# Pairwise products of the forget gates made in the projection stage, and two norms with fewer operations

## The chip, the cores and the metric

The kernel runs on one NeuronCore of a Trainium2 chip. The metric is the device time of one execution in microseconds (us); the time before is the median of three runs. Engines are named as in the profile: PE is TensorE, PEld its weight loads, DVE VectorE, ACT ScalarE, POOL GpSimd and SP SyncE, whose queue issues nearly all DMAs.

## The reference, cut to what matters

One step of a hybrid backbone of two layers, for 2048 latent and 256 context tokens (2304 in all, width 1024). A layer normalises and modulates its input, projects it, runs four mixers (differential attention, S5, HGRN2 and latent attention, MLA), gates them and projects back. The change touches HGRN2's gates, and the norm and the softmax of MLA:

```python
log_f = jnp.log(lb + (1.0 - lb) * jax.nn.sigmoid(z))   # forget gate f, per head, channel, direction
k = (1.0 - lb) * jax.nn.sigmoid(-z)
...
b = jnp.cumsum(gc, axis=1)
decay = jnp.exp(jnp.where(causal, b[:, :, None] - b[:, None, :], -jnp.inf))
scores = jnp.einsum("bthd,btshd,bshd->bhts", qc, decay, kc)
...
q = (rms_norm(cq) * P["mla_q_norm"][l].astype(F32)).astype(dt) @ P["mla_w_uq"][l]
ckv_n = (rms_norm(ckv) * P["mla_kv_norm"][l].astype(F32)).astype(dt)
...
p = jax.nn.softmax(s, axis=-1).astype(v.dtype)
return jnp.einsum("bhqk,bkhd->bqhd", p, v)
```

The decay between two tokens of a chunk of 64 is the product of the gates between them.

## The kernel before

Both layers run the same stages. `first_stage` projects keys, queries and values of differential attention (`proj1`, blocks of 384 tokens). In `mixers`, `proj2` makes the rest of the projection in four token groups of 576, each in two halves of 288 columns; it is woven with the differential attention that is already running, and TensorE's order in it is that of the program text. Then the remaining attention (differential, then MLA) is woven with `ssm()`, that is HGRN and after it S5. `out_proj` closes the layer. Outside TensorE's order in `proj2` a planner orders each engine's queue, by its own costs and by priorities; it places an operation as soon as its inputs are there by its reckoning, and the engines then issue in that order.

In `proj2` the blocks of `FB2` go one after another: 24 matmuls of 288 columns for each half, then `evac2`. Four of the blocks are `hf`, a head's gate pre-activations of both directions (64 + 64 rows). Line 393 clamps them out of PSUM, lines 394 to 396 are ScalarE's, line 397 makes k and line 398 the gate f in the tile `evf`, which goes to the DRAM tensor `HF` (line 399); k goes to `PF` (line 403). GpSimd meanwhile splits the next block's weights into a high and a low part (`split2`, lines 171 and 173).

`mla_up` in the same stage norms by `rs_bc`: a sum of squares by matmul, a logarithm and an exponential on ScalarE, one Newton step on VectorE (lines 594 to 597).

`hgrn` takes a head in five groups of up to 512 tokens (40 groups over two layers; the last of a head has 256). A group loads F (the gates, line 1035), X and Y (q and k of both directions). The decay inside a chunk of 64 is made by doubling: at level `lev` blocks of 2^lev tokens are paired, the second block's X and the first block's Y are multiplied by a gate product of the other block (lines 1059, 1060), and `T2`, made from the pairs of `T` (line 1062), is the gate product of the joined block. The six products of a group are a chain of their own: they need F alone. The last goes into `td` (lines 1095, 1096) for the scan over the chunks. Three groups can be in flight (`HB`).

MLA's second pass divides by the sum of the exponentials with one Newton step (lines 984 to 989). S matrices of the attention rotate through four PSUM banks.

Of the kernel before, what the change touches and what calls it, by code (L numbers as in the profile page):

```python
# [10 lines left out]
F32 = mybir.dt.float32  # L11
# [5 lines left out]
ALU = mybir.AluOpType  # L17
# [9 lines left out]
NT = LS + LC  # L27
# [79 lines left out]


PR = (0, 0)
AVB = 2  # L110
PPB = 3
DA_A = 740
# [269 lines left out]
def evac2(g, l, p, kind, idx, ps, tok0, n):  # L382
    nc = g.nc
    sl = slice(tok0, tok0 + n)
    o = p.tile([128, n], F32, tag="ev", name="ev", bufs=EVB)
    if kind == "u":
        nc.scalar.copy(o.rearrange("p (s j) -> p s j", s=8), ps.rearrange("p (j s) -> p s j", s=8))
        nc.sync.dma_start(g.UD[idx * 128:(idx + 1) * 128, :, tok0 // 8:(tok0 + n) // 8], o.rearrange("p (s j) -> p s j", s=8))
        return
    if kind == "hf":  # L390
        om, lb = g.omlb[:, l, idx:idx + 1], g.lb[:, l, idx:idx + 1]
        f = p.tile([128, n], F32, tag="evf", name="evf")
        nc.vector.tensor_scalar(o, ps, -80.0, None, ALU.max)
        nc.scalar.activation(out=o, in_=o, func=AF.Exp, scale=-1.0)
        nc.scalar.activation(out=f, in_=o, func=AF.Ln, bias=1.0)
        nc.scalar.activation(out=f, in_=f, func=AF.Exp, scale=-1.0)
        nc.vector.scalar_tensor_tensor(o, o, om, f, ALU.mult, ALU.mult)
        nc.vector.tensor_scalar(f, f, om, lb, ALU.mult, ALU.add)
        nc.sync.dma_start(g.HF[idx, :, sl], f)
    else:  # L400
        nc.scalar.copy(o, ps)
    dst, r0 = (g.GX, GIDX[kind] + idx * 128) if kind in GIDX else (g.PF, FROW[(kind, idx)])
    nc.sync.dma_start(dst[r0:r0 + 128, sl], o)
# [102 lines left out]
def proj2(g, l):  # L506
    nc = g.nc
    G, H = 576, 288
    with ExitStack() as es:
        pa = es.enter_context(pool(g, "p2a", 1, "right"))  # L510
        p = es.enter_context(pool(g, "p2", 2, "right"))
        ph = es.enter_context(pool(g, "p2h", 1, "right"))
        pu = es.enter_context(pool(g, "mu", 1, "right"))
        for t0 in range(0, NT, G):
            hi, lo = [], []
            for b in range(2):
                bs = slice(t0 + b * H, t0 + (b + 1) * H)
                for j, x in enumerate((hi, lo)):
                    t = (pa, ph)[b].tile([128, 8, H], F32R, tag=f"h{j}{b}", name="h2")
# [3 lines left out]
                if b == 0 and t0 == 0:  # L523
                    yield GS0
                    w = mla_up_weights(g, l, ph)
# [37 lines left out]

            def ups():
                if t0 == 0:
                    ck = pu.tile([128, H], F32, tag="ckc", name="ckc")
                    nc.sync.dma_start(ck[:, :256], g.A["cmc"][l])
                    yield from mla_kv(g, l, w, pu, ck, NT, 256)
                for b in range(2):
                    yield from mla_up(g, l, w, pu, cks[b], cqs[b], t0 + b * H, H)  # L570
# [11 lines left out]
def rs_bc(g, p, sqs, n, inv_n):  # L582
    nc = g.nc
    ps = pst(g, "mm", "psrb")
    for i, s in enumerate(sqs):
        k = s.shape[0]
        nc.tensor.matmul(ps[:, :n], lhsT=g.ones[:k, :], rhs=s, start=(i == 0), stop=(i == len(sqs) - 1))
    a = p.tile([128, 288], F32, tag="rba", name="rba")[:, :n]
    y = p.tile([128, 288], F32, tag="rby", name="rby")[:, :n]
    t = p.tile([128, 288], F32, tag="rbt", name="rbt")[:, :n]  # L590
    nc.vector.tensor_scalar(a, ps[:, :n], inv_n, EPS, ALU.mult, ALU.add)
    nc.scalar.activation(out=y, in_=a, func=AF.Ln)
    nc.scalar.activation(out=y, in_=y, func=AF.Exp, scale=-0.5)
    nc.vector.tensor_tensor(t, y, y, ALU.mult)
    nc.vector.tensor_tensor(t, t, a, ALU.mult)
    nc.vector.tensor_scalar(t, t, -0.5, 1.5, ALU.mult, ALU.add)
    nc.vector.tensor_tensor(y, y, t, ALU.mult)
    return y


# [287 lines left out]
def mla(g, l, p):  # L888
    nc = g.nc
# [46 lines left out]
    def pass2(pr, qb):  # L936
        n, _, kts = key_blocks(qb)
# [4 lines left out]
        av = pst(g, "av", "psmav")  # L942
# [39 lines left out]
        rc = g.pm.tile([128, 512], F32, tag="mrc", name="mrc")  # L982
        tq = g.pm.tile([128, 512], F32, tag="mtq", name="mtq")
        nc.scalar.activation(out=rc[:, :n], in_=pd[:, :n], func=AF.Ln)
        nc.scalar.activation(out=rc[:, :n], in_=rc[:, :n], func=AF.Exp, scale=-1.0)
        nc.vector.tensor_tensor(tq[:, :n], pd[:, :n], rc[:, :n], ALU.mult)
        nc.vector.tensor_scalar(tq[:, :n], tq[:, :n], -1.0, 2.0, ALU.mult, ALU.add)
        nc.vector.tensor_tensor(rc[:, :n], rc[:, :n], tq[:, :n], ALU.mult)
        nc.vector.tensor_tensor(rc[:, :n], av[:, :n], rc[:, :n], ALU.mult)
        nc.sync.dma_start(g.MX[768 + pr * 128:768 + (pr + 1) * 128, qb * 512:qb * 512 + n], rc[:, :n])  # L990
        yield 1

# [3 lines left out]
def hgrn(g, l, p, p1):  # L996
    nc = g.nc
# [10 lines left out]
    for xs, n, nm in ((ks, 6, "hks"), (qz, 2 * HB, "hqz")):  # L1008
        for i in range(n):
            t = p1.tile([128, 512], F32, name=f"{nm}{i}")  # L1010
# [19 lines left out]
    def group(k, h, c0, nch):  # L1030
# [2 lines left out]
        r0, z0 = FROW[("hq", h // 2)] + (h % 2) * 64, FROW[("hf", h)]  # L1033
        F, X, Y = (p.tile([128, 512], F32, tag=t, name="h" + t, bufs=n)[:, :W] for t, n in (("F", 3), ("X", HB), ("Y", HB)))
        nc.sync.dma_start(F, g.HF[h, :, sl])
        nc.sync.dma_start(Y[0:64], g.PF[z0:z0 + 64, sl])
        nc.sync.dma_start(X[64:128], g.PF[z0 + 64:z0 + 128, sl])
        nc.sync.dma_start(X[0:64], g.PF[r0:r0 + 64, sl])
# [6 lines left out]
        nc.vector.tensor_tensor(X[0:64], X[0:64], F[0:64], ALU.mult)  # L1045
        nc.vector.tensor_tensor(Y[64:128], Y[64:128], F[64:128], ALU.mult)
        nc.vector.tensor_tensor(Av, ps[:, :W // 2].rearrange("p (c t) -> p c t", t=64), g.id64.unsqueeze(1).to_broadcast([128, nch, 64]), ALU.mult)
        T = F
        for lev in range(6):
            m = 1 << lev  # L1050
            nb = W // (2 * m)
            K_, Q_ = ks[lev], qz[k % HB * 2 + lev % 2]
            xx, yy, kz, qq = (t_[:, :W].rearrange("p (b t m) -> p b t m", t=2, m=m) for t_ in (X, Y, K_, Q_))
            nc.scalar.copy(kz[0:64, :, 0, :], yy[0:64, :, 0, :])
            nc.scalar.copy(kz[64:128, :, 1, :], xx[64:128, :, 1, :])
            nc.scalar.copy(qq[0:64, :, 1, :], xx[0:64, :, 1, :])
            nc.scalar.copy(qq[64:128, :, 0, :], yy[64:128, :, 0, :])
            Tv = T.rearrange("p (b t) -> p b t", t=2)
            nc.vector.tensor_tensor(xx[:, :, 1, :], xx[:, :, 1, :], Tv[:, :, 0:1].to_broadcast([128, nb, m]), ALU.mult)
            nc.vector.tensor_tensor(yy[:, :, 0, :], yy[:, :, 0, :], Tv[:, :, 1:2].to_broadcast([128, nb, m]), ALU.mult)  # L1060
            T2 = p.tile([128, 256 >> lev], F32, tag=f"T{lev}", name=f"T{lev}")[:, :nb]
            nc.vector.tensor_tensor(T2, Tv[:, :, 0], Tv[:, :, 1], ALU.mult)
            T = T2
            ps = pst(g, "mm", "pshg")
            pairs(ps, K_, Q_, nch)
            nc.vector.copy_predicated(Av, g.masks[:, lev, :].bitcast(U32).unsqueeze(1).to_broadcast([128, nch, 64]),
                                      ps[:, :W // 2].rearrange("p (c t) -> p c t", t=64))
            yield 2.5
        nc.scalar.copy(QF[0:64, sl], X[0:64])
        nc.scalar.copy(QF[64:128, sl], Y[64:128])  # L1070
        pt = pst(g, "mm", "pskt")
# [624 lines left out]
def build(nc, tc, A, O, depth=DEPTH):  # L1696
    with ExitStack() as es:
# [7 lines left out]
        g.ED = dp.tile([2, 128, 16, 257], F32, name="ED")  # L1705
        g.X1 = dp.tile([NT, D], F32, name="X1")
        g.PF = dp.tile([1120, NT], F32, name="PF")
        g.HF = dp.tile([4, 128, NT], F32, name="HF")
        g.GX = dp.tile([D, NT], F32, name="GX")
        g.KRD = dp.tile([2, 34, NK], F32, name="KRD")  # L1710
# [97 lines left out]
```

## Time and profile before

| what | value |
|---|---|
| median of three runs | 5299.3 us (5298.6 to 5303.79) |
| profiled execution, its own time | 5296.69 us |
| its span, first to last instruction | 5294.9 us |
| mean granted TensorE clock | 0.935 |
| TensorE, VectorE, ScalarE, GpSimd busy | 89%, 72%, 60%, 21% |

The profile is of one execution. The stages of layer 0 lie at 0 to 464 us (`first_stage`), 464 to 1537 (`proj2` with attention), 1537 to 2056 (HGRN with attention), 2056 to 2380 (S5 with attention) and from there to 2716 (the end of the attention and `out_proj`); those of layer 1 begin at 2716, 3097, 4184, 4686 and 4973. Busy time is the time in which an engine executes; its idle time costs something only where it lies on the chain of work that ended last.

### The profile page before, as it was taken

What the parts mean: (1) busy time and instruction counts of PE and PEld (TensorE: products, weight loads), DVE (VectorE), ACT (ScalarE), POOL (GpSimd) and SP (SyncE); (2) the same over time, 40 slices, a digit from 0 to 9 for tenths busy, and PEclk for the clock granted to TensorE, in tenths of its full rate; (3) what the DMA queues carried; (4) which work ended last, traced back from release to release, by engine and by line L of the source; (5) the groups of instructions that cost most, each with busy time, mean ns of one, the idle gap of its engine ahead of it and who ended that gap; (6) DMA issues with size and microseconds to landing.
All of it is one profiled execution on the core that took longest, in us unless ns stands there. A gap on an engine that the chain in (4) does not pass through costs nothing.

```text
span 5294.9 us, 81097 instructions
## 1 busy us (share of the span) xinstructions
PE 4724.9 (89%) x27920; PEld 3434.4 (65%) x27920; DVE 3835.7 (72%) x7616; ACT 3183.3 (60%) x7516; POOL 1089.4 (21%) x1323
## 2 busy tenths in 40 slices
PE   6787999999998997898987879999999989989899
PEld 5676767677665664445776757676776656654477
DVE  7655767676668886896676657676766688879877
ACT  3225878777777783235433258787777777743354
POOL 4651222222210000000227712222222100000022
PEclk8998999999998997899999989999999989989999
DMA  6555233433332124415445452334333321241253
GB/s 219 170 174 154 87 105 96 130 116 104 92 88 75 47 57 129 130 50 148 157 155 200 159 167 86 108 94 130 116 103 93 88 73 48 54 117 52 75 155 126
DMA packets 507523, 599.37 MB, mean 113 GB/s; under 512 B 147630, under 2 KB 414806, under 8 KB 507110
## 3 DMA queue, kind: packets, MB, share of 16 engines
q1 hardware_dynamic: 506630, 592.61, 37.3%
q8 instruction: 220, 3.60, 0.3%
q14 instruction: 193, 1.58, 0.1%
q0 software_dynamic: 480, 1.57, 0.1%
HBM read 378.42 MB, written 215.18 MB: 112 GB/s over the span
## 4 chain that ended last, share of the span: by engine, by line
PE 49%; DVE 18%; DMA 13%; ACT 10%; issue 4%; POOL 4%; SPq 1%; ACTq 0%; DVEq 0%; POOLq 0%
PE psav L858 5%; PE psS L870 4%; PE psF L177 4%; PE psF L178 4%; PE psF L179 4%; PE psS L817 4%; PE psmav L950 3%; ACT junk L820 3%; PE psM L961 2%; DVE nm L818 2%; DVE a L872 2%; DVE mnm L927 2%; ACT pp L871 2%; PE psM L926 2%; PE pshg L1018 2%
## 5 line engine op out<-in xcount | busy, mean ns | idle before, releaser
L818 DVE TENSOR_REDUCE nm<-psS 128x1 f32<-128x512 f32 (+1 forms) x1312 | 790.5, 626 | 351.7 <-PE psS L817 340.5
L820 ACT ACTIVATE junk<-psS,nm 128x512 bf16<-128x512 f32 (+1 forms) x1312 | 848.7, 647 | 202.2 <-DVE nm L818 182.4
L871 ACT ACTIVATE pp<-psS 128x512 f32<-128x512 f32 (+1 forms) x1184 | 654.5, 594 | 165.7 <-PE psS L870 159.6
L177 PE MATMUL psF<-h,whi 128*128 128x288 f32 x2304 | 697.9, 303 | 32.8 <-ACT whi L169 32.8
L872 DVE SCALAR_TENSOR_TENSOR a<-pp,nlam 128x512 f32<-128x512 f32 (+1 forms) x592 | 510.3, 864 | 257.6 <-ACT pp L871 256.9
L178 PE MATMUL psF<-h,whi 128*128 128x288 f32 x2304 | 687.9, 299 | 0.0
L179 PE MATMUL psF<-h,wlo 128*128 128x288 f32 x2304 | 685.1, 297 | 1.8 <-DVE wlo L173 1.8
L964 ACT ACTIVATE me<-psM 128x512 f32<-128x512 f32 (+1 forms) x592 | 345.6, 590 | 440.8 <-PE psM L963 395.1
L817 PE MATMUL psS<-ks,qs 96*128 96x512 f32 (+1 forms) x1312 | 544.5, 425 | 58.9 <-ACT junk L820 37.7
L870 PE MATMUL psS<-qs,ks 98*128 98x512 f32 (+1 forms) x1184 | 440.6, 436 | 53.9 <-ACT junk L820 38.7
L177 PEld LDWEIGHTS psF<-h,whi 128*128 128x128 f32 x2304 | 444.7, 193 | 65.3 <-ACT whi L169 34.5
L171 POOL CAST whi<-w 128x1024 fp32r<-128x1024 f32 x140 | 153.2, 1094 | 1622.0 <-PE psF L178 1299.7
L178 PEld LDWEIGHTS psF<-h,whi 128*128 128x128 f32 x2304 | 444.8, 193 | 54.8
L927 DVE TENSOR_REDUCE mnm<-psM 128x1 f32<-128x512 f32 (+1 forms) x656 | 394.1, 623 | 70.9 <-PE psM L926 69.0
L179 PEld LDWEIGHTS psF<-h,wlo 128*128 128x128 f32 x2304 | 441.5, 192 | 3.1 <-DVE wlo L173 3.1
L817 PEld LDWEIGHTS psS<-ks,qs 96*128 96x128 f32 x1312 | 255.2, 197 | 165.5 <-ACT junk L820 98.4
L870 PEld LDWEIGHTS psS<-qs,ks 98*128 98x128 f32 x1184 | 203.3, 192 | 236.3 <-ACT junk L820 136.4
L173 POOL TENSOR_TENSOR wlo<-w,whi 128x1024 fp32r<-128x1024 f32 x140 | 350.3, 2502 | 11.2
L967 DVE TENSOR_TENSOR macc<-macc,me 128x1024 f32<-128x1024 f32 x256 | 311.2, 1216 | 45.0 <-ACT me L964 44.2
L950 PE MATMUL psmav<-me,mv 128*64 128x512 f32 (+1 forms) x1184 | 318.0, 631 | 13.7 <-ACT me L964 7.9
L858 PE MATMUL psav<-a,dav 128*64 128x512 f32 (+1 forms) x1184 | 309.5, 643 | 18.2 <-DVE a L872 18.2
L961 PE MATMUL psM<-qs,ks 98*128 98x512 f32 (+1 forms) x592 | 269.8, 456 | 49.2 <-ACT me L964 21.6
(451 smaller groups left out, 10191.2 us busy)
## 6 DMA issues: line engine op xcount, KB each, us to landing
w<-wF SPq DMA_DIRECT2D x152, 512.0 KB
h<-HD SPq DMA_DIRECT2D x64, 576.0 KB
wmod<-w_mod SPq DMA_DIRECT2D x48, 512.0 KB
HD<-hhi SPq DMA_DIRECT2D x12, 1536.0 KB
HD<-hlo SPq DMA_DIRECT2D x12, 1536.0 KB
GX<-ev SPq DMA_DIRECT2D x128, 144.0 KB
gt<-GX SPq DMA_DIRECT2D x36, 512.0 KB
PF<-ev SPq DMA_DIRECT2D x96, 144.0 KB
```

What stands on the lines that cost most here:

```text
L177: nc.tensor.matmul(out, lhsT=w_hi, rhs=x_hi, start=start, stop=False)
L178: nc.tensor.matmul(out, lhsT=w_hi, rhs=x_lo, start=False, stop=False)
L179: nc.tensor.matmul(out, lhsT=w_lo, rhs=x_hi, start=False, stop=stop)
L817: nc.tensor.matmul(ps[:, :kn], lhsT=qs[0:96, i, t * 128:(t + 1) * 128], rhs=key_cols(ks[i], k0, kn)[0:96], start=True, stop=True)
L818: nc.vector.tensor_reduce(nm[:, i, t, ci:ci + 1], ps[:, :kn], axis=AX.X, op=ALU.max, negate=True)
L820: nc.scalar.activation(out=junk[:, :kn], in_=ps[:, :kn], func=AF.Exp, bias=nm[:, i, t, ci:ci + 1], accum_out=sm[:, i, t, ci:ci + 1])
L858: x = nc.tensor.matmul(av[hh * 64:(hh + 1) * 64, :n], lhsT=v[:, kt, hh * 64:(hh + 1) * 64], rhs=aa[:, hh, :n], start=(ki == 0), stop=(ki = ...
L870: nc.tensor.matmul(ps[:, :n], lhsT=key_cols(ks[2 * hh + m], kt * 128, 128), rhs=qs[:, 2 * hh + m, :n], start=True, stop=True)
L871: nc.scalar.activation(out=pp[:, m, :n], in_=ps[:, :n], func=AF.Exp)
L872: last = nc.vector.scalar_tensor_tensor(aa[:, hh, :n], pp[:, 1, :n], nlam, pp[:, 0, :n], ALU.mult, ALU.add)
L927: nc.vector.tensor_reduce(nm[:, i, t, ci:ci + 1], ps[:, :kn], axis=AX.X, op=ALU.max, negate=True)
L950: x = nc.tensor.matmul(av[i * 64:(i + 1) * 64, :n], lhsT=v[:, kts[ki], i * 64:(i + 1) * 64], rhs=e[:, i, :n], start=(ki == 0), stop=(ki == ...
```

## The change

Of the six gate products of a group, those of levels 0 to 4 are made in `evac2`, right behind the gate f, for 288 tokens at a time: five dependent VectorE operations with 144, 72, 36, 18 and 9 results in each partition, in a tile `evt` with one buffer. They are stored in a new DRAM tensor `HT`, in rows of 31 numbers for each 32 tokens. `hgrn` loads them with each group into a tile with two buffers (`HTB`) and keeps only the last product, from the 16 numbers in place 30. In `rs_bc` and in MLA's second pass three operations are written as two, with SCALAR_TENSOR_TENSOR. The tile `ckc` shares the buffer of `sq2`.

```diff
--- before.py
+++ after.py
@@ -107,6 +107,7 @@
 
 
 PR = (0, 0)
+HTB = 2
 AVB = 2
 PPB = 3
 DA_A = 740
@@ -397,6 +398,14 @@
         nc.vector.scalar_tensor_tensor(o, o, om, f, ALU.mult, ALU.mult)
         nc.vector.tensor_scalar(f, f, om, lb, ALU.mult, ALU.add)
         nc.sync.dma_start(g.HF[idx, :, sl], f)
+        nb = n // 32
+        tt = p.tile([128, nb, 32], F32, tag="evt", name="evt", bufs=1)
+        src, a = f.rearrange("p (k c) -> p k c", c=32), 0
+        for w in (16, 8, 4, 2, 1):
+            s2 = src.rearrange("p k (b t) -> p k b t", t=2)
+            nc.vector.tensor_tensor(tt[:, :, a:a + w], s2[:, :, :, 0], s2[:, :, :, 1], ALU.mult)
+            src, a = tt[:, :, a:a + w], a + w
+        nc.sync.dma_start(g.HT[idx, :, tok0 // 32:tok0 // 32 + nb, 0:31], tt[:, :, 0:31])
     else:
         nc.scalar.copy(o, ps)
     dst, r0 = (g.GX, GIDX[kind] + idx * 128) if kind in GIDX else (g.PF, FROW[(kind, idx)])
@@ -563,7 +572,7 @@
 
             def ups():
                 if t0 == 0:
-                    ck = pu.tile([128, H], F32, tag="ckc", name="ckc")
+                    ck = pu.tile([128, 2, H], F32, tag="sq2", name="ckc")[:, 0, :]
                     nc.sync.dma_start(ck[:, :256], g.A["cmc"][l])
                     yield from mla_kv(g, l, w, pu, ck, NT, 256)
                 for b in range(2):
@@ -592,9 +601,8 @@
     nc.scalar.activation(out=y, in_=a, func=AF.Ln)
     nc.scalar.activation(out=y, in_=y, func=AF.Exp, scale=-0.5)
     nc.vector.tensor_tensor(t, y, y, ALU.mult)
-    nc.vector.tensor_tensor(t, t, a, ALU.mult)
-    nc.vector.tensor_scalar(t, t, -0.5, 1.5, ALU.mult, ALU.add)
-    nc.vector.tensor_tensor(y, y, t, ALU.mult)
+    nc.vector.scalar_tensor_tensor(t, t, -0.5, a, ALU.mult, ALU.mult)
+    nc.vector.scalar_tensor_tensor(y, t, 1.5, y, ALU.add, ALU.mult)
     return y
 
 
@@ -984,9 +992,8 @@
         nc.scalar.activation(out=rc[:, :n], in_=pd[:, :n], func=AF.Ln)
         nc.scalar.activation(out=rc[:, :n], in_=rc[:, :n], func=AF.Exp, scale=-1.0)
         nc.vector.tensor_tensor(tq[:, :n], pd[:, :n], rc[:, :n], ALU.mult)
-        nc.vector.tensor_scalar(tq[:, :n], tq[:, :n], -1.0, 2.0, ALU.mult, ALU.add)
-        nc.vector.tensor_tensor(rc[:, :n], rc[:, :n], tq[:, :n], ALU.mult)
-        nc.vector.tensor_tensor(rc[:, :n], av[:, :n], rc[:, :n], ALU.mult)
+        nc.vector.scalar_tensor_tensor(rc[:, :n], tq[:, :n], 2.0, rc[:, :n], ALU.subtract, ALU.mult)
+        nc.vector.scalar_tensor_tensor(rc[:, :n], av[:, :n], -1.0, rc[:, :n], ALU.mult, ALU.mult)
         nc.sync.dma_start(g.MX[768 + pr * 128:768 + (pr + 1) * 128, qb * 512:qb * 512 + n], rc[:, :n])
         yield 1
 
@@ -1033,6 +1040,8 @@
         r0, z0 = FROW[("hq", h // 2)] + (h % 2) * 64, FROW[("hf", h)]
         F, X, Y = (p.tile([128, 512], F32, tag=t, name="h" + t, bufs=n)[:, :W] for t, n in (("F", 3), ("X", HB), ("Y", HB)))
         nc.sync.dma_start(F, g.HF[h, :, sl])
+        ht = p.tile([128, 16, 32], F32, tag="ht", name="hht", bufs=HTB)[:, :W // 32]
+        nc.sync.dma_start(ht[:, :, 0:31], g.HT[h, :, c0 * 4:c0 * 4 + W // 32, 0:31])
         nc.sync.dma_start(Y[0:64], g.PF[z0:z0 + 64, sl])
         nc.sync.dma_start(X[64:128], g.PF[z0 + 64:z0 + 128, sl])
         nc.sync.dma_start(X[0:64], g.PF[r0:r0 + 64, sl])
@@ -1045,7 +1054,6 @@
         nc.vector.tensor_tensor(X[0:64], X[0:64], F[0:64], ALU.mult)
         nc.vector.tensor_tensor(Y[64:128], Y[64:128], F[64:128], ALU.mult)
         nc.vector.tensor_tensor(Av, ps[:, :W // 2].rearrange("p (c t) -> p c t", t=64), g.id64.unsqueeze(1).to_broadcast([128, nch, 64]), ALU.mult)
-        T = F
         for lev in range(6):
             m = 1 << lev
             nb = W // (2 * m)
@@ -1055,17 +1063,25 @@
             nc.scalar.copy(kz[64:128, :, 1, :], xx[64:128, :, 1, :])
             nc.scalar.copy(qq[0:64, :, 1, :], xx[0:64, :, 1, :])
             nc.scalar.copy(qq[64:128, :, 0, :], yy[64:128, :, 0, :])
-            Tv = T.rearrange("p (b t) -> p b t", t=2)
-            nc.vector.tensor_tensor(xx[:, :, 1, :], xx[:, :, 1, :], Tv[:, :, 0:1].to_broadcast([128, nb, m]), ALU.mult)
-            nc.vector.tensor_tensor(yy[:, :, 0, :], yy[:, :, 0, :], Tv[:, :, 1:2].to_broadcast([128, nb, m]), ALU.mult)
-            T2 = p.tile([128, 256 >> lev], F32, tag=f"T{lev}", name=f"T{lev}")[:, :nb]
-            nc.vector.tensor_tensor(T2, Tv[:, :, 0], Tv[:, :, 1], ALU.mult)
-            T = T2
+            if 0 < lev < 5:
+                a, w = 32 - (64 >> lev), 32 >> lev
+                Tv = ht[:, :, a:a + w].rearrange("p k (b t) -> p k b t", t=2)
+                xk, yk = (t_.rearrange("p (k b t m) -> p k b t m", k=W // 32, t=2, m=m) for t_ in (X, Y))
+                x1, y0 = xk[:, :, :, 1, :], yk[:, :, :, 0, :]
+                ta, tb = (Tv[:, :, :, i:i + 1].to_broadcast([128, W // 32, w // 2, m]) for i in range(2))
+            else:
+                Tv = (F if lev == 0 else ht[:, :, 30]).rearrange("p (b t) -> p b t", t=2)
+                x1, y0 = xx[:, :, 1, :], yy[:, :, 0, :]
+                ta, tb = (Tv[:, :, i:i + 1].to_broadcast([128, nb, m]) for i in range(2))
+            nc.vector.tensor_tensor(x1, x1, ta, ALU.mult)
+            nc.vector.tensor_tensor(y0, y0, tb, ALU.mult)
             ps = pst(g, "mm", "pshg")
             pairs(ps, K_, Q_, nch)
             nc.vector.copy_predicated(Av, g.masks[:, lev, :].bitcast(U32).unsqueeze(1).to_broadcast([128, nch, 64]),
                                       ps[:, :W // 2].rearrange("p (c t) -> p c t", t=64))
             yield 2.5
+        T = p.tile([128, 8], F32, tag="T5", name="T5")[:, :2 * nch]
+        nc.vector.tensor_tensor(T, Tv[:, :, 0], Tv[:, :, 1], ALU.mult)
         nc.scalar.copy(QF[0:64, sl], X[0:64])
         nc.scalar.copy(QF[64:128, sl], Y[64:128])
         pt = pst(g, "mm", "pskt")
@@ -1705,6 +1721,7 @@
         g.ED = dp.tile([2, 128, 16, 257], F32, name="ED")
         g.X1 = dp.tile([NT, D], F32, name="X1")
         g.PF = dp.tile([1120, NT], F32, name="PF")
+        g.HT = dp.tile([4, 128, NT // 32, 32], F32, name="HT")
         g.HF = dp.tile([4, 128, NT], F32, name="HF")
         g.GX = dp.tile([D, NT], F32, name="GX")
         g.KRD = dp.tile([2, 34, NK], F32, name="KRD")
```

## Rows read from the trace of the kernel before

**Rows 1.** The page: each engine's busy time, and the chain by engine.

```profile
PE 4724.9 (89%) x27920; PEld 3434.4 (65%) x27920; DVE 3835.7 (72%) x7616; ACT 3183.3 (60%) x7516; POOL 1089.4 (21%) x1323
...
PE 49%; DVE 18%; DMA 13%; ACT 10%; issue 4%; POOL 4%; SPq 1%; ACTq 0%; DVEq 0%; POOLq 0%
```

**Rows 2.** Stretches: busy us of each engine, granted clock, DMA share, GB/s.

```profile
464.00:1537.00 1073.00, 996.14 (x5389) 756.22 (x5391) 737.44 (x1265) 822.75 (x2170) 252.48 (x141) 0.96 0.34 103
1537.00:2056.00 519.00, 475.59 (x4061) 311.79 (x4059) 417.57 (x962) 385.68 (x881) 9.10 (x15) 0.91 0.23 61
4686.00:4973.00 287.00, 258.00 (x1020) 135.66 (x1018) 271.13 (x534) 94.19 (x171) 0.71 (x7) 0.96 0.27 75
```

**Rows 3.** The same view: two of the eight stretches with `hf`.

```profile
525.00:594.00 69.00, 62.89 (x346) 49.52 (x344) 56.48 (x90) 55.30 (x144) 19.53 (x12) 0.98 0.29 91
1063.00:1130.00 67.00, 62.20 (x366) 50.38 (x365) 52.74 (x103) 53.89 (x152) 18.66 (x11) 1.00 0.51 149
```

**Rows 4.** Timeline, HGRN stage: start us, us, engine, line, operation.

```profile
1593.14 0.28 DVE L1062 TENSOR_TENSOR T<-T 128x128 f32<-128x128 f32 x1
...
1595.00 0.21 DVE L1062 TENSOR_TENSOR T<-T 128x64 f32<-128x64 f32 x1
...
1596.48 0.18 DVE L1062 TENSOR_TENSOR T<-T 128x32 f32<-128x32 f32 x1
...
1598.20 0.17 DVE L1062 TENSOR_TENSOR T<-T 128x16 f32<-128x16 f32 x1
...
1599.39 0.15 DVE L1062 TENSOR_TENSOR T<-T 128x8 f32<-128x8 f32 x1
```

**Rows 5.** Timeline in an `hf` stretch: GpSimd and VectorE.

```profile
534.65 2.72 POOL L173 TENSOR_TENSOR wlo<-w,whi 128x1024 fp32r<-128x1024 f32 x1
...
535.03 2.50 DVE L398 TENSOR_SCALAR evf<-evf,omlb,lb 128x288 f32<-128x288 f32 x1
```

**Rows 6.** Single lines: ns as min/median/max, first and last start.

```profile
L397 DVE SCALAR_TENSOR_TENSOR ev<-ev,omlb,evf x64: 498/509/1811, 532.2 to 4033.5; 128x288 f32<-128x288 f32 x64
...
L398 DVE TENSOR_SCALAR evf<-evf,omlb,lb x64: 407/428/2499, 535.0 to 4034.3; 128x288 f32<-128x288 f32 x64
...
L595 DVE TENSOR_TENSOR rbt<-rbt,rba x32: 444/458/2548, 530.4 to 4138.9; 128x288 f32<-128x288 f32 x32
L596 DVE TENSOR_SCALAR rbt<-rbt x32: 292/309/1031, 530.9 to 4139.4; 128x288 f32<-128x288 f32 x32
```

**Rows 7.** Groups, 464 to 1537 us: busy us, mean ns | idle before.

```profile
L397 DVE SCALAR_TENSOR_TENSOR ev<-ev,omlb,evf 128x288 f32<-128x288 f32 x32 | 19.4, 607 | 7.6 <-ACT evf L396 7.5
L398 DVE TENSOR_SCALAR evf<-evf,omlb,lb 128x288 f32<-128x288 f32 x32 | 16.4, 511 | 0.5
...
L595 DVE TENSOR_TENSOR rbt<-rbt,rba 128x288 f32<-128x288 f32 x16 | 12.4, 777 | 0.4
```

**Rows 8.** The same view of the whole span: the pairwise products.

```profile
L1062 DVE TENSOR_TENSOR T<-T 128x16 f32<-128x16 f32 (+5 forms) x200 | 38.8, 197 | 1.0
...
L1062 DVE TENSOR_TENSOR T<-hF 128x256 f32<-128x256 f32 (+1 forms) x40 | 15.8, 394 | 20.3 <-DMA hF<-HF 20.3
```

**Rows 9.** Page's packets; a store's issue; two loads on the chain.

```profile
DMA packets 507523, 599.37 MB, mean 113 GB/s; under 512 B 147630, under 2 KB 414806, under 8 KB 507110
...
L388 SPq DMA_DIRECT2D UD<-ev x32: 513/540/587, 505.8 to 3976.5; - x32
...
5170.15 3.94 DMA y<-YD
...
1605.43 2.41 DMA hF<-HF
```

**Rows 10.** SP's waits: line, waited for, us in total, times, longest.

```profile
SPq L532 <- POOL wlo L173: 198.3, 51, 20.0
```

**Rows 11.** MLA's norm: ns as min/median/max, first and last start.

```profile
L987 DVE TENSOR_SCALAR mtq<-mtq x20: 279/418/428, 1765.1 to 5031.8; 128x512 f32<-128x512 f32 x16, 128x256 f32<-128x256 f32 x4
L988 DVE TENSOR_TENSOR mrc<-mrc,mtq x20: 415/683/693, 1765.6 to 5032.3; 128x512 f32<-128x512 f32 x16, 128x256 f32<-128x256 f32 x4
```

## Prediction

> **What bounds the kernel now.** I read the totals of the page first, then the busy time of each engine stage by stage, then the chain of work that ended last, then the groups of single lines. The totals show TensorE busy for 89% of the span and VectorE for 72%, and the chain gives TensorE 49% and VectorE 18% [rows 1]. No engine is the only limit. Of VectorE's 3835.7 us some 18% of 5294.9, or 953 us, lie on the chain: one microsecond of VectorE work costs about 0.25 us of the end. That quarter is my price for VectorE work added or removed where no row says more.
>
> The change moves work between two stages, of which each layer has one; I show those of layer 0. In the first (464 to 1537 us: the second projection, woven with differential attention) TensorE is busy for 93%, VectorE for 69% and GpSimd for 24%; in the second (1537 to 2056: HGRN beside attention) it is 92%, 80% and 2% [rows 2]. The first is not even, though. Where the four `hf` blocks come out, about 68 us in each of four token groups per layer, VectorE is busy for 56.5 of 69 us and 52.7 of 67 us [rows 3]. There are eight such stretches, and the added products fall into them.
>
> **Part 1: five products per `hf` evacuation, added.** Four `hf` blocks by eight halves by two layers make 64 evacuations, each with a dependent row of five TENSOR_TENSOR, of 144, 72, 36, 18 and 9 results for each partition. The products of the old code have the same form: 0.28 us for 128 results, then 0.21, 0.18, 0.17 and 0.15 [rows 4]. A little more for the odd sizes gives 0.30 + 0.22 + 0.19 + 0.17 + 0.15 = 1.03 us. These ops have two SBUF inputs, beside a busy GpSimd. L398, with a median of 0.43 us, took 2.50 us when it began 0.4 us after a 2.72 us GpSimd subtraction, and both ended together [rows 5]. On average L398 lies 0.08 us over its median, L397 0.10 and L595 0.32 [rows 6, 7]. I take 0.09 for each of five: 0.45 us. So an evacuation costs 1.48 us, and 64 cost 95 us of VectorE. At a quarter this is +24 us. The bounds: nothing, if TensorE covers it all, and 64 times (1.03 + 5 times 0.32) = 168 us at a quarter, +42.
>
> The Trainium skill ("SBUF — State Buffer", SBUF: two separate sides) gives a rule for this: GpSimd ops and VectorE ops in a two-port mode or with two SBUF inputs share a port pair as an exclusive lock, held for the whole instruction. The trace agrees: 2.50 us beside 2.72 [rows 5], and L595, which has two SBUF inputs, reached 2.55 [rows 6]. By it only the first of the five would wait, with GpSimd's 24% as the chance and half of 2.5 us as the wait, 0.3 us in place of 0.45: +21 instead of +24. It speaks against the move, since the stage that the products leave has hardly any GpSimd work.
>
> **Part 2: the products of HGRN, removed.** Of 240 products (200 of 38.8 us and 40 of 15.8 us [rows 8]) the last of each group stays, 40 at 0.15 us: 54.6 - 6.1 = 48.5 us of VectorE go. At a quarter: -12 us; the ends are nothing, if TensorE at 92% hides it, and -39, if VectorE at 80% sets the pace of that stage by itself (80% of 48.5). The multiplications at levels 1 to 4 read the same number of elements through one more dimension; I cost that at nothing.
>
> **Part 3: what waits for the loads.** The first product of a group made VectorE wait 20.3 us in all for the load of F [rows 8]. VectorE issues in order, so the attention's reductions stood behind it. That wait can go; but the last product, which stays, needs nothing except the new load, and the planner put the first product right behind the load. So I expect the same wait on `ht`: 0, between -20 (no one waits) and +20 (it lands later than F did). The load has 2048 rows of 124 bytes. Two loads that together have as many rows of 128 bytes took 3.94 us on the chain, and a load of F took 2.41 [rows 9]. The two buffers of `ht` hardly tighten this: the older one is free at level 5 of the group two before, which the program text puts two steps ahead of level 1 of the group that loads.
>
> The "DMA: Bandwidth & Descriptors" page of the Trainium skill (Specifications) puts the line rate at rows of 512 B and over, with a read-modify-write below. The change adds 64 stores of 1152 rows and 40 loads, 147,456 short rows in all, about as many as the kernel has [rows 9]. By it the load would land late: +20 in place of 0 in part 3, and +28 for the sum. The 3.94 us lean that way; no row here shows a store of such rows on the chain.
>
> **Part 4: SP's queue.** 64 more stores at about 0.54 us (the store of UD, 1024 rows of 144 bytes [rows 9]) and loads of up to twice as many rows, an estimated 1.1 us, make some 74 us of issue. In the queue a store waits for the fifth product, and behind it stand the stores of PF and the loads of the next weights, which already wait for GpSimd [rows 10]; TensorE needs those blocks later. The products' buffer is single, so where two evacuations follow closely the next first product waits for the store before it. I take 0 for both, up to +8 together. The shared buffer of `ckc` makes the first square of the norm wait for four small matmuls that come before it anyway: 0.
>
> **Part 5: the two norms.** In `rs_bc` 0.458 + 0.309 + 0.458 become two SCALAR_TENSOR_TENSOR of about 0.509 (L397): 0.21 us less in each of 32 calls [rows 6], with one op less exposed to GpSimd, 10 us in all; the result gates TensorE's next products, so I take -3. In latent attention 0.418 + 0.683 + 0.683 become two of about 0.73 (0.683 and the 0.05 by which L397 exceeds L595): 0.32 us in each of 16 large calls [rows 11], -1.
>
> **The sum:** +24 - 12 + 0 + 0 - 3 - 1 = +8 us. On the profiled run (5296.7 us, with a span of 5294.9) that is 5304.7; that run lies 2.6 us under the median of 5299.3, so I predict 5307 against the median.
>
> **Rival, faster.** TensorE at 93% hides the products: a tenth of 95 us, +9, in place of a quarter. The waits on F go and none on `ht` follows, -20. With the other terms: 9 - 12 - 20 - 4 = -27, 5272 us. For it speaks that the load of F lies on the chain [rows 9]; against it, that the product that stays is ready as early.
>
> **Rival, slower.** The `hf` stretches saturate. Eight evacuations at 1.48 us bring 11.8 us to each: 56.5 + 11.8 = 68.3 of 69 us, and 64.5 of 67. The fullest stage has VectorE at 94% [rows 2]. At 90%, since this stage is in a fixed order on TensorE, the two take 75.9 and 71.7 us: 5.8 us more on average, eight times: +46 in place of +24. That is +30, 5329 us. It decides once the stretch needs VectorE for over some 90%; before the change it is at 82% and 79%. For it: reductions, exponentials and TensorE follow each other here. Against it: the attention's scores have four PSUM banks, so TensorE can run some matmuls ahead.
>
> **Chances.** A change of 0.2% (10.6 us) is about what a measurement here can tell. Forecast 0.43, between 5290 and 5320; faster rival 0.30, around 5272; slower rival 0.27, around 5329. Faster by over 0.2%: 0.28 of the first rival and 0.04 of the forecast, 0.32. Slower: 0.26 of the second and the upper third of the forecast, 0.15, together 0.41. The rest is 0.27. The range reaches to both rivals and as far past them as the bounds of parts 1 and 3: 5266 to 5346.
>
> **What would show it.** After the change the two second-projection stages should be longer by some 12 us each, their VectorE time by some 45 us, with single products of 0.15 us stretched beyond 1 us beside GpSimd; the HGRN stages shorter by about 6 us each, with VectorE waiting for `ht` in place of F. If the projection stages keep their length, part 1 is wrong; if VectorE waits for no load, or much longer, part 3 is. A planner that orders the other stages anew would move the time for a cause that this sum leaves out.

## The result, and the profile after

The change makes the kernel slower: 5385.6 us (5378.7 to 5388.8) against 5299.2, a ratio of 1.0169 with a 95% interval of 1.0149 to 1.0189. That is +86 us where +8 was forecast, and outside the range. The profiled execution of the changed kernel took 5378.71 us, with a span of 5376.9.

The first table of the changed kernel is the one of busy time by stretch: from and to, length, busy us (and instructions) of PE, PEld, DVE, ACT and POOL, granted clock, DMA share and GB/s. The stretches are the second projection and HGRN of layer 0, then of layer 1.

```profile
464.00:1576.00 1112.00, 1012.11 (x5389) 769.10 (x5391) 780.25 (x1409) 823.78 (x2170) 252.22 (x141) 0.95 0.36 103
1576.00:2088.00 512.00, 469.64 (x4009) 304.11 (x4006) 398.85 (x851) 380.12 (x877) 9.01 (x15) 0.92 0.29 70
3128.00:4256.00 1128.00, 1020.42 (x5398) 772.07 (x5399) 788.01 (x1417) 831.76 (x2191) 251.84 (x141) 0.94 0.37 105
4256.00:4760.00 504.00, 458.31 (x3998) 304.78 (x3995) 395.10 (x847) 378.71 (x873) 8.77 (x15) 0.92 0.30 71
```

Against [rows 2], and for layer 1 against the stage times listed under the profile before, the projection stage of layer 0 grew from 1073 to 1112 us and that of layer 1 from 1087 to 1128, which together is all but 6 us of the loss. HGRN went from 519 to 512 and from 502 to 504. VectorE's busy time in the first stage rose from 737 to 780 us, as forecast. So the added work has the size that was expected, and the two stages lost over three times what the work was priced at (80 us against 24).

The waits say what else came in. In this view each line is an engine and a line of the code, what it waited for, the total, the count and the longest wait, in us; the first two lines are VectorE's, the others SP's queue.

```profile
DVE evt L406 <- DMA HT<-evt: 51.1, 33, 5.7
DVE T L1084 <- DMA hht<-HT: 10.4, 11, 2.4
SPq L541 <- POOL wlo L174: 179.1, 46, 18.9
SPq L408 <- DVE evt L406: 162.4, 45, 9.2
```

VectorE stands 51.1 us at the first product of an evacuation until the store of the evacuation before has landed: the tile `evt` has one buffer. The wait on `ht` in HGRN, 10.4 us, is half of that on F which it replaced [rows 8]. SP's older wait for GpSimd has not grown [rows 10]. Its new wait of 162.4 us, at the store until the fifth product is done, is weighed under e9.

The timeline of VectorE around one such wait, with one operation of ScalarE (start, us, engine, line, operation; in brackets the idle time before it and its releaser), and the chain of work that ended last in the same place (start, us, what):

```profile
537.67 1.90 DVE L399 TENSOR_SCALAR evf<-evf,omlb,lb 128x288 f32<-128x288 f32 x1
...
540.46 0.29 DVE L406 TENSOR_TENSOR evt<-evf 128x144 f32<-128x144 f32 x1
...
542.54 0.22 DVE L406 TENSOR_TENSOR evt<-evt 128x72 f32<-128x72 f32 x1
...
543.71 0.18 DVE L406 TENSOR_TENSOR evt<-evt 128x36 f32<-128x36 f32 x1
...
544.18 0.41 DVE L399 TENSOR_SCALAR evf<-evf,omlb,lb 128x288 f32<-128x288 f32 x1
...
545.18 0.17 DVE L406 TENSOR_TENSOR evt<-evt 128x18 f32<-128x18 f32 x1
...
547.33 0.17 DVE L406 TENSOR_TENSOR evt<-evt 128x9 f32<-128x9 f32 x1
...
548.67 0.43 DVE L399 TENSOR_SCALAR evf<-evf,omlb,lb 128x288 f32<-128x288 f32 x1
...
549.31 0.60 ACT L879 ACTIVATE pp<-psS 128x512 f32<-128x512 f32 x1
...
550.97 0.31 DVE L406 TENSOR_TENSOR evt<-evf 128x144 f32<-128x144 f32 x1 [0.87 <-DMA HT<-evt]
551.20 0.74 DVE L880 SCALAR_TENSOR_TENSOR a<-pp,nlam 128x512 f32<-128x512 f32 x1
```

```profile
546.72 0.69 DVE nm L826
547.42 0.09 DVE evt L406
547.51 0.02 issue
547.53 3.42 DMA HT<-evt
550.95 0.02 issue
550.97 0.31 DVE evt L406
551.28 0.07 DVE a L880
```

The five products of one evacuation, 1.0 us of work, are spread over 540.46 to 547.50, because the planner puts the attention's reductions between operations that depend on each other. Then the store takes 3.42 us to land; 26 stores of `HT` lie on the chain, with 2.75 to 8.29 us each. So the one buffer is held for 10.5 us, while the next two gates are ready at 544.6 and 549.1. The first product of the next evacuation stands at the head of VectorE's queue until 550.97, and L880 behind it waits too, although the exponentials that it reads were done at 549.91. VectorE stood idle for 0.87 us here. Over all 64 evacuations the spread of the five has a median of 4.1 us (1.2 to 10.6).

On the page's chain VectorE has 19% and SP's queue 2%, a point more each than in [rows 1], and the store is a line of its own in it:

```profile
PE 48%; DVE 19%; DMA 13%; ACT 9%; issue 4%; POOL 3%; SPq 2%; ACTq 0%; DVEq 0%; POOLq 0%
PE psav L866 4%; PE psS L878 4%; PE psmav L958 4%; PE psF L178 4%; PE psF L179 3%; PE psF L180 3%; PE psS L825 3%; DVE nm L826 3%; ACT junk L828 3%; PE psM L969 2%; DVE a L880 2%; DMA HT<-evt 2%; PE pshg L1025 2%; PE psM L971 2%; PE psM L970 2%
```

Two per cent of 5377 us is about as much as was lost, but a chain only names suspects. TensorE's order in the projection stage is the text's, so it is the same in all kernels here, and lengths of this stage can be compared directly. In the mixers the planner makes the order, and it made another one for nearly every kernel; only e3 and e11 below have the same one, and e7 and e8, which take it from the text.

### The profile page after: what moved, and what is told of

Read it like the earlier page. It is cut to its first block, busy times and chain, and to the rows that moved or that the text cites. A ratio compares the mean times of both kernels' runs of the same rounds, so it can differ in the third digit from the quotient of the medians.

```text
span 5376.9 us, 81555 instructions
## 1 busy us (share of the span) xinstructions
PE 4760.0 (89%) x27920; PEld 3462.1 (64%) x27920; DVE 3890.0 (72%) x7684; ACT 3179.6 (59%) x7516; POOL 1087.8 (20%) x1323
## 4 chain that ended last, share of the span: by engine, by line
PE 48%; DVE 19%; DMA 13%; ACT 9%; issue 4%; POOL 3%; SPq 2%; ACTq 0%; DVEq 0%; POOLq 0%
PE psav L866 4%; PE psS L878 4%; PE psmav L958 4%; PE psF L178 4%; PE psF L179 3%; PE psF L180 3%; PE psS L825 3%; DVE nm L826 3%; ACT junk L828 3%; PE psM L969 2%; DVE a L880 2%; DMA HT<-evt 2%; PE pshg L1025 2%; PE psM L971 2%; PE psM L970 2%
## 5 line engine op out<-in xcount | busy, mean ns | idle before, releaser
L178 PE MATMUL psF<-h,whi 128*128 128x288 f32 x2304 | 704.6, 306 | 32.3 <-ACT whi L170 30.8
L179 PE MATMUL psF<-h,whi 128*128 128x288 f32 x2304 | 696.6, 302 | 0.0
L880 DVE SCALAR_TENSOR_TENSOR a<-pp,nlam 128x512 f32<-128x512 f32 (+1 forms) x592 | 514.4, 872 | 231.9 <-ACT pp L879 231.0
L178 PEld LDWEIGHTS psF<-h,whi 128*128 128x128 f32 x2304 | 452.3, 196 | 65.8 <-ACT whi L170 32.5
L179 PEld LDWEIGHTS psF<-h,whi 128*128 128x128 f32 x2304 | 452.7, 196 | 57.8
```

The lines of the kernel that those rows point to most:

```text
L178: nc.tensor.matmul(out, lhsT=w_hi, rhs=x_hi, start=start, stop=False)
L179: nc.tensor.matmul(out, lhsT=w_hi, rhs=x_lo, start=False, stop=False)
L880: last = nc.vector.scalar_tensor_tensor(aa[:, hh, :n], pp[:, 1, :n], nlam, pp[:, 0, :n], ALU.mult, ALU.add)
```

## The experiments

In the table the second projection is taken from its first to its last matmul in the trace, the mixers from there to the first matmul of `out_proj`; layer 0 and layer 1, in us, of the profiled execution. The last column is the median of all runs, and the ratio to the kernel before on the same chip. Where VectorE has no more to do in the projection than before (before, e3, e4, e7, e10, e11 and e12), a stage takes 1065 to 1078 us: a difference of a few us in one stage of one execution says nothing.

| kernel | second projection | mixers | whole, ratio (95%) |
|---|---|---|---|
| before | 1071, 1072 | 921, 865 | 5299.2 |
| the change | 1110, 1114 | 918, 875 | 5385.6, 1.0169 (1.0149 to 1.0189) |
| e1, two buffers | 1090, 1084 | 891, 859 | 5306.7, 1.0020 (1.0005 to 1.0036) |
| e2, products only | 1085, 1090 | 920, 872 | 5329.6, 1.0065 (1.0047 to 1.0083) |
| e3, store, no products | 1068, 1074 | 934, 879 | 5313.0, 1.0037 (1.0025 to 1.0049) |
| e4, norms only | 1073, 1065 | 908, 882 | 5294.7, 0.9996 (0.9982 to 1.0010) |
| e5, e2 and store, one buffer | 1112, 1111 | 929, 885 | 5375.9, 1.0151 (1.0120 to 1.0181) |
| e6, e2 and store, two buffers | 1102, 1100 | 921, 854 | 5332.9, 1.0060 (1.0037 to 1.0083) |
| e7, before, text order | 1078, 1076 | 1057, 1054 | 5620.1, 1.0596 (1.0564 to 1.0628) |
| e8, e1, text order | 1089, 1084 | 1053, 1048 | 5652.2, 1.0661 (1.0633 to 1.0690) |
| e9, three buffers | 1088, 1081 | 890, 874 | 5288.4, 0.9982 (0.9972 to 0.9991) |
| e10, gates on GpSimd in HGRN | 1074, 1078 | 894, 864 | 5267.4, 0.9947 (0.9932 to 0.9962) |
| e11, products on GpSimd | 1075, 1075 | 922, 872 | 5309.3, 1.0027 (1.0014 to 1.0040) |
| e12, before, other order | 1072, 1071 | 905, 883 | 5314.8, 1.0027 (1.0013 to 1.0042) |

**Two buffers (e1).**

```diff
-        tt = p.tile([128, nb, 32], F32, tag="evt", name="evt", bufs=1)
+        tt = p.tile([128, nb, 32], F32, tag="evt", name="evt", bufs=2)
...
-    t = p.tile([128, 288], F32, tag="rbt", name="rbt")[:, :n]
+    t = p.tile([128, 288], F32, tag="rpt", name="rbt")[:, :n]
```

> The changed kernel with two buffers for the products in place of one (room for the second: the temporary of the norm, rbt, shares the tag of a temporary of rope). Products, stores and loads are all there. Theory W (VectorE, at the first product of an evacuation, waits for the store of the evacuation before to land, and everything behind it on VectorE waits too): the waits end, both second-projection stages fall from 1112 and 1128 us to about 1085 and 1100, the whole to about 5325 us (5310 to 5345). Theory S (the 44 us of added VectorE work in each stage saturate the hf stretches): the stages keep their length, 5365 to 5390 us. Theory D (the store's traffic or its place in SP's queue): 5360 to 5390 us too, but the waits of VectorE for the store are gone from the trace.

5306.7 us: 75 of the 86 us are gone with one more buffer, more even than theory W asked for. Theory S falls. The wait shrinks to a quarter:

```profile
DVE evt L406 <- DMA HT<-evt: 13.3, 4, 6.2
```

But the two projection stages give back only 20 and 30 us. In the profiled executions the mixers are shorter too, by 27 and 16 us, and the buffer isn't used there (that execution of e1 lies 12 us under its median). The following runs take the two apart.

**The products alone (e2), and the store with one and two buffers (e5, e6).** In e2 the five products stand in `evac2` of the kernel before, without a store. In e5 the store is added, in e6 the store and the second buffer. HGRN and the norms are those of before in all three, and `ckc` shares the buffer of `sq2` as in the change.

```diff
         nc.sync.dma_start(g.HF[idx, :, sl], f)
+        nb = n // 32
+        tt = p.tile([128, nb, 32], F32, tag="evt", name="evt", bufs=1)
...
+            nc.vector.tensor_tensor(tt[:, :, a:a + w], s2[:, :, :, 0], s2[:, :, :, 1], ALU.mult)
+            src, a = tt[:, :, a:a + w], a + w
+        nc.sync.dma_start(g.HT[idx, :, tok0 // 32:tok0 // 32 + nb, 0:31], tt[:, :, 0:31])
```

The last line is in e5 and e6 only; e6 has `bufs=2`, with `rbt` in the tag `rpt` as in e1.

> The kernel before with the five products added to each hf evacuation (one buffer, never stored; ckc shares the buffer of the squares to make room). HGRN is as before and makes its own products, the norms are as before. Only the cost of the arithmetic. Theory W: 5299 + 24 = about 5323 us (5299 to 5341), the second-projection stage of layer 0 some 1085 us long. Theory S: both stages as long as in the changed kernel, some 1112 us, and with no gain in HGRN 5380 to 5400 us.

> The kernel of e2_products_only with the store of the products added, from the one buffer; HGRN and the norms are still as before and nothing loads what is stored. Theory W: the wait of VectorE for the store returns with all its length; the second-projection stages go from 1085 and 1090 us (e2_products_only) to some 1108 and 1115, the whole from 5330 to 5380 us (5365 to 5395). If the single buffer is not the cause: 5330 to 5340 us.

> As e5_store_one_buffer, with two buffers for the products. Theory W: no wait, as e2_products_only: stages of some 1085 and 1090 us, the whole 5330 us (5315 to 5345). Theory D (the traffic of the stores or their place in SP's queue costs by itself): 5350 us and over, whatever the buffers.

All three came within what theory W expected for the whole. The arithmetic by itself is +34 us (0.65%), +14 and +18 in the two stages. The store from one buffer brings the stages to 1112 and 1111, which is the change's own length, with nothing taken from HGRN. VectorE's wait is back (e5, then e6):

```profile
DVE evt L405 <- DMA HT<-evt: 54.5, 28, 6.2
```

```profile
DVE evt L405 <- DMA HT<-evt: 18.0, 6, 5.9
```

So the projection stages split: +32 us for the products (e2) and +48 for the store through one buffer (e5 less e2), 80 in all, where the change has 39 + 41. The profiled execution of e5 lies 21 us above its median, so the 48 us are rough; the medians put e5 46 us over e2 and 43 over e6. Set against the wait, the 48 us stand for 54.5 us, about 0.9 each. Two other pairs give 0.6 (e5 to e6: some 22 us of the stages for 36.5 of wait) and 1.3 (the change to e1: 50 for 37.8). The products are 106 us of VectorE in e2 and cost 34, about 0.3 each:

```profile
L405 DVE TENSOR_TENSOR evt<-evt 128x72 f32<-128x72 f32 (+3 forms) x256 | 73.4, 287 | 2.1
L405 DVE TENSOR_TENSOR evt<-evf 128x144 f32<-128x144 f32 x64 | 32.8, 513 | 0.3
```

Why a microsecond of this wait is two to four times as dear isn't settled by a run. What the rows show is that a wait falls where the queue behind it is full, as L880 at 551.20, while the planner slots a product between reductions. The single buffer also changes VectorE's order: the first product begins 3.7 us after its gate in the median of the change and 0.8 us after it in e1. So a part of the 48 us may be the planner's placing and not the wait. In e6 the whole agrees with e2, but its stages are 16 and 10 us longer with 18 us of wait left, where the expectation had them as long as e2's, and in the trace its mixers make up for it; that part isn't explained.

**Three buffers (e9).** As e1 with `bufs=3`; `rby` shares a tag as well.

> The changed kernel with three buffers for the products (rbt and rby share the tags of rope's temporaries). In the trace of e1_two_buffers VectorE still waits 13.3 us in all for the store of the products, 4 times. Theory W: that ends and the whole comes to 5297 us (5288 to 5307), 10 us under e1_two_buffers. Theory D: no change from e1_two_buffers, 5307 us, since what is left then is the cost of the products and of the traffic.

5288.4 us, at the lower end of theory W, and 0.18% faster than before (0.09 to 0.28%). No wait for the store is left in the trace, and no store of `HT` lies on the chain (26 in the change, 2 in e1). TensorE's order is nearly that of e1, so the 18 us between the two may be the rest of the wait, which was 13.3 us, and noise; the traces don't show it, since the projection is only 5 us shorter in e9 and its mixers are 14 us longer, in an execution that lies 16 us above the median. All of the change's transfers are in this kernel, and SP still waits for the fifth product:

```profile
SPq L408 <- DVE evt L406: 80.1, 34, 8.0
```

Its projection stages are some 25 us longer than before, less than e2's 32 for the products alone. So theory D, that the stores or their place in SP's queue cost by themselves, finds nothing here.

**The store without the products (e3).**

```diff
-            nc.vector.tensor_tensor(tt[:, :, a:a + w], s2[:, :, :, 0], s2[:, :, :, 1], ALU.mult)
...
-        nc.sync.dma_start(g.HT[idx, :, tok0 // 32:tok0 // 32 + nb, 0:31], tt[:, :, 0:31])
+        nc.sync.dma_start(g.HT[idx, :, tok0 // 32:tok0 // 32 + nb, 0:31], f.rearrange("p (k c) -> p k c", c=32)[:, :, 0:31])
```

> The changed kernel without the five products: the store writes the first 31 of 32 columns of f instead (f has two buffers), HGRN loads that and multiplies by it (its output is then not the reference's). All added DMAs and all that is taken from HGRN and the norms are there; the added arithmetic and its single buffer are not. Theory W and theory S: the second-projection stages are 1073 and 1087 us as in the kernel before, the whole 5299 - 9 (HGRN, as in the trace of the changed kernel) - 4 (norms) = about 5286 us (5270 to 5300). Theory D: the stages stay at 1112 and 1128, 5360 us and over.

The stages came as theories W and S said, 1068 and 1074: 64 stores of short rows cost the projection nothing. The whole is a miss: 5313 in place of 5286. The mixers are 14 us longer than before in each layer, although VectorE has less to do there.

**The products on GpSimd (e11).** In e1, `nc.vector.tensor_tensor(tt...)` becomes `nc.gpsimd.tensor_tensor(tt...)`.

> The kernel of e1_two_buffers with the five products of an evacuation on GpSimd. VectorE loses the added 44 us in each second-projection stage; GpSimd's split of the next weights waits behind the products. If the arithmetic on VectorE is what is left of the loss: stages back at 1073 us, the whole 5307 - 30 = 5277 us (5265 to 5290). If GpSimd's queue (products waiting for the gate or the store ahead of the split) holds up the weights: stages of 1085 us and over, 5305 us and over.

Half right: the stages are back at 1075, so VectorE's part was what was left of the loss, and GpSimd's wait for gates and stores holds up no weights. The whole is still 5309. This kernel has exactly the TensorE order of e3, instruction by instruction, and agrees with it within 4 us. That fits a loss that goes with the order. Yet in the two traces the mixers of e11 are 12 and 7 us shorter than those of e3, at a mean granted clock of 0.91 and 0.92 against 0.89 and 0.90: so much moves in single executions with no change of order.

**The order in the mixers (e4, e7, e8, e12).** e4 has the two norms only; e7 and e8 are before and e1 with TensorE's order in the mixers from the text (`MAN = True`); e12 is before with `YW = 1040` in place of 1000.

> The kernel before with the fewer operations in the two norms, nothing else. By the prediction 4 us less: 5295 us (5285 to 5300). If the planner or the places on VectorE move by the edit alone, anything between 5285 and 5315 us, and that is then the size of what the other runs can't tell apart.

> The kernel before, with TensorE's order in the mixers taken from the program text in place of the planner (the switch MAN). A base for e8_two_buffers_text_order; its own time may lie anywhere from 5250 to 5450 us, the second-projection stages stay at 1071 and 1072 us.

> The kernel of e1_two_buffers with TensorE's order in the mixers from the program text, the same as in e7_before_text_order. The second-projection stages should stand 18 and 11 us over those of e7 as in e1. Theory H (HGRN without its products is really some 30 us shorter in each layer, as in the trace of e1_two_buffers): the mixers after the second projection are 30 us shorter in each layer than in e7, and the whole 30 us or more under e7. Theory P (the planner found a better order in e1_two_buffers by luck, and the removed 48 us of VectorE are worth a quarter at most): the mixers are 0 to 8 us shorter in each layer, and the whole is 10 to 25 us over e7.

> The kernel before with one number of the weave of attention with HGRN and S5 moved by 4% (YW 1000 to 1040): the same instructions, in another order of the planner's in the mixers. Theory P (the planner's order alone moves the mixers by 20 to 30 us, which is why e1_two_buffers is 30 us shorter there than the changed kernel and e3_store_no_products 20 us longer than expected): the second-projection stages stay at 1071 and 1072 us, the mixers after them move by 10 to 30 us in one of the layers, either way; the whole 5275 to 5325 us, but not within 3 us of 5296. If the order is worth nothing: 5296 us, 3 us either way, and mixers as before.

e12 does the same work as before in another order and is 17 us slower (0.13 to 0.42%): theory P's range, and about the size of e3's miss. Its profiled execution is the fastest of ten, so its stages don't show the median's loss, only that the mixers moved, by -15 and +18 us. e4 is no different from before by its time, and its mixers moved by -13 and +17. Moves of this size in one trace aren't proof of the order's worth: e3 and e11, with one order, differ by 12 and 7 us, and e1 and e9, with nearly one order, by 1 and 15. What carries theory P is the median of e12, 17 us by an order alone.

The stretch of HGRN in layer 0 differs as well: the changed kernel has a stretch of 512 us for it, e1 and e9 have 481 and 480, with the same HGRN operations and nearly the same order of TensorE in the latter two.

```profile
1555.00:2036.00 481.00, 440.21 (x3903) 294.98 (x3903) 380.16 (x827) 374.95 (x866) 9.46 (x15) 0.92 0.30 73
```

```profile
1556.00:2036.00 480.00, 439.86 (x3906) 293.16 (x3904) 381.25 (x828) 376.39 (x869) 9.51 (x15) 0.93 0.31 73
```

Fewer TensorE instructions lie in these stretches than the 4009 of the changed kernel: another share of the attention is put beside HGRN. Theory H, that HGRN without its products is 30 us shorter, falls with e8. In one fixed order the mixers of e8 are shorter than those of e7 by 4 and 6 us. Its medians put e8 32 us over e7, past theory P's 10 to 25. The profiled execution of e7 lies 20 us above its median and that of e8 9 below, so the 4 and 6 us are uncertain by about as much; that they are not 30 is certain.

**HGRN's products on GpSimd (e10).** The kernel before with the new norms, and one word changed in HGRN.

```diff
-            nc.vector.tensor_tensor(T2, Tv[:, :, 0], Tv[:, :, 1], ALU.mult)
+            nc.gpsimd.tensor_tensor(T2, Tv[:, :, 0], Tv[:, :, 1], ALU.mult)
```

> The kernel before with the fewer operations in the norms, and with the six products of a group made in HGRN as before, on GpSimd in place of VectorE; nothing in the projection, no store and no load added. VectorE is freed of 54 us in HGRN, beside a GpSimd that is busy for 2% there. With the price of the prediction (a quarter): 5299 - 14 - 4 = 5281 us (5270 to 5292). If VectorE's time in HGRN is worth nothing: 5295 us. If the products come late from GpSimd, or its hold on the shared port slows VectorE: 5300 us and over.

5267.4 us, 0.53% faster than before (0.38 to 0.68%), the fastest kernel of the case and a little past the expectation. GpSimd needs 0.42 us for a product of levels 1 to 5, and VectorE is rid of them without doing them elsewhere:

```profile
L1060 POOL TENSOR_TENSOR T<-T 128x32 f32<-128x32 f32 (+5 forms) x200 | 83.7, 422 | 104.1 <-DVE hY L1058 90.9 <-DVE hX L1057 1.6
```

How much of the 28 us is the freed VectorE and how much a better order, given that order alone moves 17, stays open.

## Why the prediction was wrong

**The step that failed is in part 4**: "The products' buffer is single, so where two evacuations follow closely the next first product waits for the store before it. I take 0 for both, up to +8 together." The mechanism was named and its price was not worked out. It is 48 us in the projection stages (e5 less e2), and 43 to 46 by the medians: five to six times the bound. Two of the numbers for it were at hand. [rows 3] has eight evacuations in 69 us, one in 8.6 on average. The loads of y on the chain took 3.94 us [rows 9], near the 3.42 that the store took. What was missing is the third number, the time from the first to the last of five dependent operations in a queue that holds other work: with the 1.48 us of part 1, which is busy time alone, 1.48 + 3.94 = 5.4 fits well into 8.6. The queue spreads them over 4.1 us in the median and up to 10.6, and the gates come unevenly (544.6 and 549.1 above). Then a buffer is held for 7.5 us as a rule, often for longer than the next gate takes to come: VectorE waited at 33 of the 64 first products.

**Part 1, the products: right in kind, too low.** +24 was forecast, between 0 and +42; e2 has +34. Busy time was 95 us by forecast and is 106 in e2, with single products stretched to 2.4 us as expected. The price is 0.32 in place of 0.25. The slower rival's saturation gave +46 for the same part; the truth lies between the two, and the 5329 us of that rival belong to e2 by chance only, since e2 hasn't the gains that the rival counts in.

**Part 2, HGRN's products: not contradicted, and not visible.** VectorE's busy time in HGRN fell by 19 us in layer 0 ([rows 2] against the first table). HGRN was 7 us shorter there and 2 longer in layer 1, against 6 forecast in each; the text order gives 4 and 6 over the mixers, uncertain by some 30. The mixers of the change as a whole are 7 us longer than before, where 13 less were forecast with part 5. The last sentence of the prediction, on a planner that orders other stages anew, names what hides it: orders differ by more than this term.

**Part 3, the wait for the load: within its bounds.** It was 20.3 us on F and is 10.4 on `ht` (0 forecast, between -20 and +20). The Trainium skill's page "DMA: Bandwidth & Descriptors" (Specifications), with its read-modify-write for rows under 512 B, pointed to +20 here. The trace doesn't bear out that price: VectorE waited half as long for 2048 rows of 124 B as it had for F, and in e3 the stages with all these stores are as long as before. That a single load of such rows lands later isn't refuted: on the chain three loads of `ht` took 3.63 to 6.10 us, where eleven of F in the kernel before took 2.41 to 4.30.

**Part 4, SP's issue: smaller than feared.** A store was taken at 0.54 us and a load at 1.1; the line of the tile `hht` and that of the store show 0.37 for both, 39 us in place of 74, and in e9 it costs nothing that can be measured.

```profile
L1044 SPq DMA_DIRECT2D hht<-HT x40: 371/377/581, 1576.4 to 4695.8; - x40
L408 SPq DMA_DIRECT2D HT<-evt x64: 370/371/389, 547.5 to 4120.3; - x64
```

**Part 5, the norms:** -4 forecast; e4 has -1 (-10 to +5). It can't be told from nothing.

With the buffer out of the way the forecast of 5307 stands beside e1's 5306.7. That agreement is partly luck: e1's projection stages lost 30 us, not 24, and its mixers won 36 in a trace 12 us under the median, where 13 were forecast; the rest goes, as far as the runs tell, to an order that nobody foresaw. The faster rival, 5272 us, had products hidden by TensorE and no wait on `ht`; the products are not hidden.

## What to carry to other kernels

A buffer is held from its first write to the landing of its store, and in an in-order queue shared with other work the first write and the last can lie several times their busy time apart: set that whole hold (here 4.1 us in the median and 10.6 at most, and some 3.4 more for the landing) against the spacing of the uses, at its narrowest and not on average, before a single buffer is priced at nothing. A microsecond of wait at the head of a full queue cost 0.6 to 1.3 us of the stage here, where a microsecond of work slotted into the same queue cost 0.3. Where a planner orders a stage, change its order alone once and see what that moves: 17 us here, more than four of the five parts of this sum.

## What the hardware showed that was not expected

The issue of a DMA didn't go by its number of rows: a store of 1152 rows of 124 bytes took 0.37 us, a load of up to 2048 such rows 0.38, and a store of 1024 rows of 144 bytes 0.54 [rows 9]. GpSimd's products of 144 results in each partition took 0.43 us in e11 where VectorE's took 0.30, so at this size the slower engine is only 1.4 times slower:

```profile
L406 POOL TENSOR_TENSOR evt<-evf x64: 422/428/982, 535.9 to 4050.1; 128x144 f32<-128x144 f32 x64
```

```profile
L406 DVE TENSOR_TENSOR evt<-evf x64: 284/299/2439, 538.5 to 4043.2; 128x144 f32<-128x144 f32 x64
```

The first line is e11's, the second e1's (minimum, median and maximum in ns).
